# Weight sums of a recursive matrix product: added by accumulating transfers in place of GpSimd, activation differences on VectorE in place of GpSimd

## The chip, the core and the metric

The kernel runs on one core of one Trainium2 chip. The metric is the device time of one execution in microseconds (us); lower is better. Of before there are three timed runs and one profiled execution. Engines are named as in the profile: PE is TensorE (matmuls; PEld its weight loads), DVE is VectorE, ACT is ScalarE, POOL is GpSimd, SP is SyncE, which issues the plain transfers.

## The reference, cut to what matters

One layer of a streaming encoder: attention, a spatial gating branch, a merge, and then a squared-ReLU MLP. All is float32, with 512 tokens and a model width of 2048. The change touches the last product alone:

```
D_MODEL = 2048; SEQ = 512; D_FF = 4 * D_MODEL
h2 = rms_norm(x, g_ff[l])
x = x + jnp.square(jax.nn.relu(h2 @ w_ff1[l])) @ w_ff2[l]
```

`w_ff2` is 8192 x 2048. The kernel computes the product with it by a 2x2 recursive scheme that needs seven block products in place of eight, at the price of sums of weight blocks and differences of activation blocks.

## The kernel before, in words

**Split numbers.** Each float32 operand is split into a high and a low part (`split_to`, L101): ACT casts it to `w_hi` (L103), DVE subtracts that from the operand and gets `w_lo` (L104). A product is then three matmuls (`mm3`, L66 to L70): high by high (L68), low weight by high (L69 for the products named here), high by low (L70). The DVE subtraction needs ACT's cast, and the matmuls need both.

**First product of the MLP.** `hidden` (L597) makes 256 columns of the hidden layer: four loads of `w_ff1` (512 KB each, L87), four splits (L90 on ACT, L92 on DVE), 96 matmuls named `f`, then two evacuations (L603 on DVE, L604 on ACT) into `relu`.

**Second product.** The hidden layer is walked in 16 chunks `f` of 512 rows (L632). For each chunk, `factors` (L610) is called for two pairs of `relu` tiles: four differences of 128x256 each on POOL (L615 to L618, tiles `m`), then seven splits of 128x256 (tiles `ys`, ACT L103 and DVE L104). For each half `g` of the output columns, `strassen` (L140) loads four quarters of a 512x1024 piece of `w_ff2` (512 KB each, L156), and makes seven products of 12 matmuls each (tiles `q`). The names of the products are those of the activation factor: y11, y21, m7, m6, y22, m4, m5. Four of them need a sum of weight quarters, made on POOL (`plus`, L165, 128x1024 each) just ahead of the split: m7 takes w11+w21, m6 that sum and w22 (into a tile of its own, `w_sum`), y22 the latter and w12, m5 w21+w22. Each product is evacuated as soon as its 12 matmuls are done: DVE adds or subtracts the PSUM bank from two or four tiles `x` in SBUF (L643, 128x512). Three of the seven products share one bank, so a bank is read by DVE before the next product that adds to it.

**What sets the order.** Each engine runs its own instructions in order. The program is written in the order just told and then put in order by a scheduler that works from its own estimate of times, so an instruction of a later product can stand ahead of one of an earlier. `ahead` (L638) puts `hidden` of chunk f+1, half g, ahead of `strassen` of chunk f, half g; so PE alternates 96 `f` matmuls and 84 `q` matmuls, and the differences and `ys` splits of chunk f+1 fall into `strassen` of chunk f, g=1. Below, "the g=0 call" and "the g=1 call" are these two. In the last chunk there is no `hidden` left, and the last two calls follow the one before them directly.

**Buffers.** `w_hi` and `w_lo` of both products share six buffers, three pairs (`piece`, and `weight` at L89): the split of a product can begin when the third product before it has left PE. The quarters and `w_sum` share five buffers (`whole`, L590). The raw tiles of `w_ff1` have three of their own.

Of the kernel before, what the change touches and what calls it, by code (L numbers as in the profile page):

```python
# [12 lines left out]
ALU = mybir.AluOpType  # L13
AX = mybir.AxisListType

P = 128
# [11 lines left out]
W = 512  # L28
# [5 lines left out]
def tile_hybrid_layer(ctx: ExitStack, tc: tile.TileContext, x, g_mix, w_in, g_q, g_k, ln_g, ln_b,  # L34
# [4 lines left out]
    nc = tc.nc  # L39
# [10 lines left out]
    def slot(name, dt=F32, pool=slots):  # L50
        return pool.tile([P, 512], dt, name=name, tag="slot")
# [10 lines left out]
    def f32(ap):  # L62
        return ap.bitcast(F32)


    def mm3(o, lh, rh, start, stop, **kw):  # L66

        nc.tensor.matmul(o, lhsT=lh[0], rhs=rh[0], start=start, stop=False, **kw)  # L68
        nc.tensor.matmul(o, lhsT=lh[0], rhs=rh[1], start=False, stop=False, **kw)  # L69
        nc.tensor.matmul(o, lhsT=lh[1], rhs=rh[0], start=False, stop=stop, **kw)  # L70

    state = {"load": None}
# [22 lines left out]
    def split(src, name, scale=None, pool=slots):  # L95

        hi, lo = slot(name + "_hi", F32R, pool), slot(name + "_lo", F32R, pool)
        split_to(hi, lo, src, scale)
        return hi, lo

    def split_to(hi, lo, src, scale=None):  # L101
        if scale is None:
            nc.scalar.copy(out=hi, in_=src)  # L103
            nc.vector.tensor_tensor(out=lo, in0=src, in1=f32(hi), op=ALU.subtract)  # L104
        else:
            nc.scalar.activation(out=hi, in_=src, func=AF.Copy, scale=scale)
            nc.vector.scalar_tensor_tensor(out=lo, in0=src, scalar=scale, in1=f32(hi),
                                           op0=ALU.mult, op1=ALU.subtract)
# [31 lines left out]
    def strassen(wap, r0, c0, lhs, evac):  # L140

        KH = 2

        def piece(name):
            return wpool.tile([P, KH, W], F32R, name=name, tag="w_piece", bufs=6)

        def whole(name):
            return state["whole"].tile([P, KH, W], F32, name=name, tag="whole")

        def quarter(h, c):
            raw = whole("w_raw")
            state["load"] = nc.sync.dma_start(  # L156
                out=raw, in_=wap[r0:r0 + 2 * KH * P, c0 + c * W:c0 + (c + 1) * W]
                .rearrange("(k h p) c -> h p k c", p=P, h=2)[h])
            return raw

        w11, w12, w21, w22 = quarter(0, 0), quarter(1, 0), quarter(0, 1), quarter(1, 1)
        sc = whole("w_sum")

        def plus(o, a, b):
            nc.gpsimd.tensor_tensor(out=o, in0=a, in1=b, op=ALU.add)  # L165


        made = {"m7": lambda: plus(w11, w11, w21), "m6": lambda: plus(sc, w11, w22),
                "y22": lambda: plus(w12, sc, w12), "m5": lambda: plus(w21, w21, w22)}
        take = {"y11": w11, "y21": w12, "m7": w11, "m6": sc, "y22": w12, "m4": w22, "m5": w21}  # L170
        banks = {}
        for name, b, first, last in (("y11", 0, True, False), ("y21", 1, True, True),
                                     ("m7", 2, True, False), ("m6", 0, False, False),
                                     ("y22", 1, True, True), ("m4", 2, False, True),
                                     ("m5", 0, False, True)):
            if name in made:
                made[name]()
            hi, lo = piece("w_hi"), piece("w_lo")
            split_to(hi, lo, take[name])
            if first:  # L180
                banks[b] = [(aux if b == 1 else acc)("q") for _ in range(2)]
            for t in range(2):
                o = banks[b][t]
                for k in range(KH):
                    y = [part[:, t * P:(t + 1) * P] for part in lhs(k, name)]
                    mm3(o, y, (hi[:, k, :], lo[:, k, :]), first and k == 0, k == KH - 1,
                        skip_group_check=True)
                evac(name, t, o)
# [210 lines left out]
    for half in range(2):  # L399
# [4 lines left out]
                 lambda tb, o, v=v: v.append(split(o, "v", rstd[:, tb:tb + 1])), "v")  # L404
# [82 lines left out]
    with tc.issue_after(ref.ins):  # L487
        ws, bs = [], []
        for half in range(2):
            t = slot("ws")  # L490
            nc.sync.dma_start(out=t.rearrange("p (g j) -> p g j", g=4),
                              in_=w_sp[0, half * 4:half * 4 + 4].rearrange("g i j -> i g j"))
# [117 lines left out]
    def factors(act):  # L610

        y11, y12, y21, y22 = act[0][:, :HS], act[0][:, HS:], act[1][:, :HS], act[1][:, HS:]
        ta, tb = slot("m"), slot("m")
        m7, m6, m4, m5 = ta[:, :HS], ta[:, HS:], tb[:, :HS], tb[:, HS:]
        nc.gpsimd.tensor_tensor(out=m7, in0=y12, in1=y22, op=ALU.subtract)  # L615
        nc.gpsimd.tensor_tensor(out=m6, in0=m7, in1=y11, op=ALU.subtract)
        nc.gpsimd.tensor_tensor(out=m4, in0=y21, in1=m6, op=ALU.add)
        nc.gpsimd.tensor_tensor(out=m5, in0=y11, in1=y12, op=ALU.subtract)  # L618
        y = {}
        for name, src in (("y11", y11), ("y21", y21), ("m7", m7), ("m6", m6), ("y22", y22),  # L620
                          ("m4", m4), ("m5", m5)):
            t = slot("ys", F32R)
            y[name] = (t[:, :HS], t[:, HS:])
            split_to(*y[name], src)
        return y
# [6 lines left out]
    for f in range(chunks):  # L632
        ys = [factors(act) for act in ahead]
        ahead = []
        for g in range(2):

            if f < chunks - 1:
                ahead.append(hidden(f + 1, g))  # L638

            def evac_y(name, t, o):  # L640
                for half, c, op in takes[name]:
                    a = x2[2 * half + t, 2 * g + c]
                    nc.vector.tensor_tensor(out=a, in0=a, in1=o, op=op)  # L643
                    if f == chunks - 1 and (name, half, c) in (("m4", 0, 1), ("y21", 0, 0),
                                                              ("m5", 1, 1), ("m5", 1, 0)):
                        tb, j = 2 * half + t, 2 * g + c
                        nc.sync.dma_start(out=out[tb * P:(tb + 1) * P, j * W:(j + 1) * W], in_=a)

            strassen(w_ff2[0], f * PAIRS * 2 * P, g * 2 * W, lambda k, name: ys[k][name], evac_y)
# [25 lines left out]
```

## Time and profile before

| What | Value |
|---|---|
| median of 3 runs | 2575.06 us (2574.0 to 2575.1) |
| the profiled execution's own time | 2574.17 us |
| its span, first to last instruction | 2572.5 us |
| granted PE clock | 1.000 |
| PE busy | 2532.1 us of the span |
| DVE busy | 1438.7 us |
| ACT busy | 852.9 us |
| POOL busy | 589.0 us |
| moved by transfers | 259.83 MB, 101 GB/s on average |

How to read it: a row of a group has the line of the code, the engine, the operation, output and input by name, shape, count, the busy time and the mean duration of one in ns, and behind the bar the idle time just before these instructions with what ended it. In the timeline a row has start, duration, engine and line; a figure in square brackets is the idle time of the engine before it and what ended that. The durations of matmuls overlap, since they are pipelined; their starts follow each other at the true pace. From a transfer's issue to its landing is told by a view of its own.

### The profile page before, as it was taken

Reading aid. Unit: us, or ns where it says so; the run is one execution under the profiler, and the core shown is the slowest. Engines: PE = TensorE matmul, PEld = TensorE weight load, DVE = VectorE, ACT = ScalarE, POOL = GpSimd, SP = SyncE. Lnnn points to the kernel's source line nnn. Section 1 sums busy time; section 2 is a strip of 40 time slices with the busy share of each in tenths; the row PEclk is TensorE's granted clock in tenths of the full one; section 3 lists DMA queues with packets and bytes.
Section 4 is the critical chain, followed back from the end, with each engine's and each line's share of the span. In section 5 each row is a group of like instructions: output and inputs, shape, how many; then the busy total and the mean of one; then the engine's idle time right before and its main releaser. Section 6 shows DMA issues by size and latency. Waiting matters only on the chain.

```text
span 2572.5 us, 28610 instructions
## 1 busy us (share of the span) xinstructions
PE 2532.1 (98%) x11306; PEld 2082.1 (81%) x11306; DVE 1438.7 (56%) x1806; ACT 852.9 (33%) x1172; POOL 589.0 (23%) x379
## 2 busy tenths in 40 slices
PE   8999999999999999999999999999999999999998
PEld 7888888888888888888878777887778777877786
DVE  4555563333335333333475767667666767576759
ACT  5333342222223222223333333333332334233333
POOL 0211110000211000100223242414342333324244
PEclk9999999999999999999999999999999999999999
DMA  5332323333332333434233323233323333332323
GB/s 172 90 91 74 90 64 99 93 97 98 115 115 78 99 101 93 129 107 133 88 110 95 115 87 111 89 115 97 101 90 107 102 95 99 98 115 82 114 68 121
DMA packets 169574, 259.83 MB, mean 101 GB/s; under 512 B 8368, under 2 KB 77024, under 8 KB 169440
## 3 DMA queue, kind: packets, MB, share of 16 engines
q1 hardware_dynamic: 169440, 258.01, 32.7%
q8 instruction: 89, 1.46, 0.2%
q14 instruction: 45, 0.37, 0.0%
HBM read 253.78 MB, written 4.19 MB: 100 GB/s over the span
## 4 chain that ended last, share of the span: by engine, by line
PE 87%; DVE 10%; issue 1%; ACT 1%; DMA 0%; POOL 0%; SPq 0%; DVEq 0%; ACTq 0%; POOLq 0%
PE f L69 9%; PE f L68 9%; PE f L70 9%; PE q L69 6%; PE q L70 6%; PE q L68 6%; DVE w_lo L104 4%; DVE ys L104 3%; DVE x L643 3%; PE xo L70 2%; PE xo L69 2%; PE xo L68 2%; PE gb L68 2%; PE gb L70 2%; PE gb L69 2%; PE ga L68 2%
## 5 line engine op out<-in xcount | busy, mean ns | idle before, releaser
L92 DVE TENSOR_TENSOR w_lo<-w_raw,w_hi 128x1024 fp32r<-128x1024 f32 x336 | 414.2, 1233 | 686.5 <-ACT w_hi L90 677.7
L90 ACT CAST w_hi<-w_raw 128x1024 fp32r<-128x1024 f32 x336 | 353.7, 1053 | 988.8 <-PE q L69 190.0
L104 DVE TENSOR_TENSOR w_lo<-w_raw,w_hi 128x1024 fp32r<-128x1024 f32 x192 | 281.9, 1469 | 255.8 <-ACT w_hi L103 255.8
L68 PE MATMUL f<-h2T_hi,w_hi 128*128 128x512 f32 x1024 | 398.6, 389 | 0.0
L69 PE MATMUL f<-h2T_lo,w_hi 128*128 128x512 f32 x1024 | 398.5, 389 | 0.0
L70 PE MATMUL f<-h2T_hi,w_lo 128*128 128x512 f32 x1024 | 397.9, 391 | 0.0
L69 PE MATMUL q<-w_lo,ys 128*128 128x512 f32 x896 | 352.8, 394 | 26.4 <-DVE w_lo L104 26.3
L165 POOL TENSOR_TENSOR w_raw<-w_raw 128x1024 f32<-128x1024 f32 x64 | 183.1, 2862 | 820.0 <-DVE w_lo L104 820.0
L70 PE MATMUL q<-w_hi,ys 128*128 128x512 f32 x896 | 349.0, 389 | 0.0
L643 DVE TENSOR_TENSOR x<-x,q 128x512 f32<-128x512 f32 x512 | 331.0, 676 | 2.3 <-PE q L70 0.6
L103 ACT CAST w_hi<-w_raw 128x1024 fp32r<-128x1024 f32 x192 | 201.8, 1053 | 391.2 <-PE f L69 290.3
L68 PE MATMUL q<-w_hi,ys 128*128 128x512 f32 x896 | 324.0, 391 | 1.5 <-DVE x L643 1.2
L69 PEld LDWEIGHTS q<-w_lo,ys 128*128 128x128 f32 x896 | 168.1, 188 | 74.1 <-DVE w_lo L104 40.0
L70 PEld LDWEIGHTS f<-h2T_hi,w_lo 128*128 128x128 f32 x1024 | 192.2, 188 | 44.2 <-DVE w_lo L92 4.6
L69 PEld LDWEIGHTS f<-h2T_lo,w_hi 128*128 128x128 f32 x1024 | 192.2, 188 | 40.1
L68 PEld LDWEIGHTS f<-h2T_hi,w_hi 128*128 128x128 f32 x1024 | 192.3, 188 | 39.4
L68 PEld LDWEIGHTS q<-w_hi,ys 128*128 128x128 f32 x896 | 168.1, 188 | 40.3 <-issue 3.5
L70 PEld LDWEIGHTS q<-w_hi,ys 128*128 128x128 f32 x896 | 168.3, 188 | 33.8
L68 PE MATMUL gb<-hT_hi,w_hi 128*128 128x512 f32 x256 | 100.3, 392 | 0.2 <-DVE gb L413 0.2
L68 PE MATMUL xo<-w_hi,mT_hi 128*128 128x512 f32 x256 | 100.5, 393 | 0.0
L68 PE MATMUL ga<-hT_hi,w_hi 128*128 128x512 f32 x256 | 100.4, 392 | 0.0
L69 PE MATMUL ga<-hT_lo,w_hi 128*128 128x512 f32 x256 | 100.0, 391 | 0.0
(199 smaller groups left out, 3919.4 us busy)
## 6 DMA issues: line engine op xcount, KB each, us to landing
w_raw<-in_w_ff_dram SPq DMA_DIRECT2D x256, 512.0 KB, 3.7
w_raw<-in_w_in_dram SPq DMA_DIRECT2D x144, 512.0 KB, 3.7
w_raw<-in_w_out_dram SPq DMA_DIRECT2D x32, 512.0 KB, 3.7
w_raw<-in_w_oa_dram SPq DMA_DIRECT2D x16, 512.0 KB, 3.7
w_raw<-in_w_ob_dram SPq DMA_DIRECT2D x16, 512.0 KB, 3.6
x<-in_x_dram SPq DMA_DIRECT2D x16, 256.0 KB, 5.3
out_dram<-x SPq DMA_DIRECT2D x16, 256.0 KB, 2.2
xq<-in_x_dram SPq DMA_DIRECT2D x12, 256.0 KB, 6.4
```

The lines of the kernel that those rows point to most:

```text
L68: nc.tensor.matmul(o, lhsT=lh[0], rhs=rh[0], start=start, stop=False, **kw)
L69: nc.tensor.matmul(o, lhsT=lh[0], rhs=rh[1], start=False, stop=False, **kw)
L70: nc.tensor.matmul(o, lhsT=lh[1], rhs=rh[0], start=False, stop=stop, **kw)
L90: nc.scalar.copy(out=hi, in_=raw)
L92: nc.vector.tensor_tensor(out=lo, in0=raw, in1=f32(hi), op=ALU.subtract)
L103: nc.scalar.copy(out=hi, in_=src)
L104: nc.vector.tensor_tensor(out=lo, in0=src, in1=f32(hi), op=ALU.subtract)
L165: nc.gpsimd.tensor_tensor(out=o, in0=a, in1=b, op=ALU.add)
L643: nc.vector.tensor_tensor(out=a, in0=a, in1=o, op=op)
```

## The change

`plus` no longer adds two tiles on POOL. It issues a transfer on POOL's queue that reads a quarter of `w_ff2` from memory again and adds it to the destination tile in SBUF (`accum_op=ALU.add`). A tile `sa` is loaded with w11 (a second load of w11, plain, on SP); w21 is added to it (for m7), then, once m7's split has read it, w22 (for m6), then, once m6's split has read it, w12 (for y22). A tile `sb` is loaded with w21, and w22 added to it (for m5). One call thus has five plain loads on SP in place of four, and four accumulating transfers on POOL's queue in place of four POOL additions. The seven products come in another order: m7, y11, y21, m6, m4, y22, m5. The four differences of `factors` move from POOL to DVE.

```diff
+        def rows(h, c):
+            return wap[r0:r0 + 2 * KH * P, c0 + c * W:c0 + (c + 1) * W].rearrange("(k h p) c -> h p k c", p=P, h=2)[h]
...
-        w11, w12, w21, w22 = quarter(0, 0), quarter(1, 0), quarter(0, 1), quarter(1, 1)
-        sc = whole("w_sum")
-
-        def plus(o, a, b):
-            nc.gpsimd.tensor_tensor(out=o, in0=a, in1=b, op=ALU.add)
-
-
-        made = {"m7": lambda: plus(w11, w11, w21), "m6": lambda: plus(sc, w11, w22),
-                "y22": lambda: plus(w12, sc, w12), "m5": lambda: plus(w21, w21, w22)}
-        take = {"y11": w11, "y21": w12, "m7": w11, "m6": sc, "y22": w12, "m4": w22, "m5": w21}
+        def plus(o, h, c):
+
+            nc.gpsimd.dma_start(out=o, in_=rows(h, c), accum_op=ALU.add)
+
+
+        sa, w11, w12 = quarter(0, 0), quarter(0, 0), quarter(1, 0)
+        plus(sa, 0, 1)
+        w22, sb = quarter(1, 1), quarter(0, 1)
+        plus(sb, 1, 1)
+        take = {"y11": w11, "y21": w12, "m7": sa, "m6": sa, "y22": sa, "m4": w22, "m5": sb}
         banks = {}
-        for name, b, first, last in (("y11", 0, True, False), ("y21", 1, True, True),
-                                     ("m7", 2, True, False), ("m6", 0, False, False),
-                                     ("y22", 1, True, True), ("m4", 2, False, True),
+        for name, b, first, last in (("m7", 2, True, False), ("y11", 0, True, False),
+                                     ("y21", 1, True, True), ("m6", 0, False, False),
+                                     ("m4", 2, False, True), ("y22", 1, True, True),
                                      ("m5", 0, False, True)):
-            if name in made:
-                made[name]()
             hi, lo = piece("w_hi"), piece("w_lo")
             split_to(hi, lo, take[name])
+            if name in ("m7", "m6"):
+                plus(sa, 1, 1 if name == "m7" else 0)
...
-        nc.gpsimd.tensor_tensor(out=m7, in0=y12, in1=y22, op=ALU.subtract)
-        nc.gpsimd.tensor_tensor(out=m6, in0=m7, in1=y11, op=ALU.subtract)
-        nc.gpsimd.tensor_tensor(out=m4, in0=y21, in1=m6, op=ALU.add)
-        nc.gpsimd.tensor_tensor(out=m5, in0=y11, in1=y12, op=ALU.subtract)
+        nc.vector.tensor_tensor(out=m7, in0=y12, in1=y22, op=ALU.subtract)
+        nc.vector.tensor_tensor(out=m6, in0=m7, in1=y11, op=ALU.subtract)
+        nc.vector.tensor_tensor(out=m4, in0=y21, in1=m6, op=ALU.add)
+        nc.vector.tensor_tensor(out=m5, in0=y11, in1=y12, op=ALU.subtract)
```

Three places show how the instructions move; all are from the call of chunk f=13, g=1 (the tile numbers differ between the kernels, and the line numbers by one behind L153).

POOL's queue before, in that call: the four sums, then the eight differences of both pairs.

```order
L165 TENSOR_TENSOR w_raw_17260<-w_raw_17260,w_raw_17264 128x1024
L165 TENSOR_TENSOR w_sum_17268<-w_raw_17260,w_raw_17266 128x1024
L165 TENSOR_TENSOR w_raw_17264<-w_raw_17264,w_raw_17266 128x1024
L165 TENSOR_TENSOR w_raw_17262<-w_sum_17268,w_raw_17262 128x1024
L615 TENSOR_TENSOR m_17409<-relu_16977,relu_16980 128x256
L618 TENSOR_TENSOR m_17410<-relu_16977 128x256
```

And now: 17287 is `sa` of this call and 17296 its `sb`; 17619 is `sa` of the next call.

```order
L164 DMA w_raw_17296<-in_w_ff2_dram 128x2x512
L164 DMA w_raw_17287<-in_w_ff2_dram 128x2x512
L164 DMA w_raw_17619<-in_w_ff2_dram 128x2x512
L164 DMA w_raw_17287<-in_w_ff2_dram 128x2x512
L164 DMA w_raw_17628<-in_w_ff2_dram 128x2x512
```

The queue holds transfers alone now, and the third addition to `sa` (the fourth row, for y22) stands behind the first addition to the next call's `sa`.

DVE before, from the two evacuations of `hidden` to the split of m6 (`w_lo` from `w_sum`):

```order
L603 SCALAR_TENSOR_TENSOR relu_17254<-f1_17132,rstd_b_103 128x512
L603 SCALAR_TENSOR_TENSOR relu_17257<-f1_17133,rstd_b_103 128x512
L104 TENSOR_TENSOR w_lo_17311<-w_raw_17260,w_hi_17310 128x1024
L643 TENSOR_TENSOR x2_7982<-x2_7982,q_17273 128x512
L643 TENSOR_TENSOR x2_7984<-x2_7984,q_17274 128x512
L104 TENSOR_TENSOR w_lo_17332<-w_sum_17268,w_hi_17331 128x1024
```

And now, where 17341 is the split of y21 and 17361 that of m6:

```order
L604 SCALAR_TENSOR_TENSOR relu_17281<-f1_17159,rstd_b_103 128x512
L604 SCALAR_TENSOR_TENSOR relu_17284<-f1_17160,rstd_b_103 128x512
L616 TENSOR_TENSOR m_17437<-relu_17003,relu_17006 128x256
L619 TENSOR_TENSOR m_17438<-relu_17003 128x256
L104 TENSOR_TENSOR w_lo_17341<-w_raw_17291,w_hi_17340 128x1024
L617 TENSOR_TENSOR m_17437<-m_17437,relu_17003 128x256
L644 TENSOR_TENSOR x2_8286<-x2_8286,q_17304 128x512
L644 TENSOR_TENSOR x2_8288<-x2_8288,q_17305 128x512
L618 TENSOR_TENSOR m_17438<-relu_17006,m_17437 128x256
L104 TENSOR_TENSOR w_lo_17361<-w_raw_17287,w_hi_17360 128x1024
```

Four differences now stand on DVE ahead of m6's split; the evacuations in between are m7's where they were y11's.

PE before, where y22 begins (17350 is its `w_hi`, 17331 that of m6): it follows on the whole of m6.

```order
L69 MATMUL q_17274<-w_lo_17332,ys_16843 128x512
L70 MATMUL q_17274<-w_hi_17331,ys_16843 128x512
L68 MATMUL q_17354<-w_hi_17350,ys_16819 128x512
L68 MATMUL q_17355<-w_hi_17350,ys_16819 128x512
L69 MATMUL q_17354<-w_lo_17351,ys_16819 128x512
```

And now (17397 is y22's `w_hi`, 17360 m6's, 17379 m4's):

```order
L68 MATMUL q_17304<-w_hi_17379,ys_16848 128x512
L68 MATMUL q_17305<-w_hi_17379,ys_16848 128x512
L68 MATMUL q_17325<-w_hi_17360,ys_16842 128x512
L69 MATMUL q_17325<-w_lo_17361,ys_16842 128x512
L70 MATMUL q_17325<-w_hi_17360,ys_16842 128x512
L68 MATMUL q_17325<-w_hi_17360,ys_16869 128x512
L69 MATMUL q_17325<-w_lo_17361,ys_16869 128x512
L70 MATMUL q_17325<-w_hi_17360,ys_16869 128x512
L68 MATMUL q_17401<-w_hi_17397,ys_16845 128x512
L69 MATMUL q_17304<-w_lo_17380,ys_16848 128x512
```

y22's first matmul is now the 51st of the call: 48 of m7, y11, y21 and m6 and two of m4 stand ahead of it, and m4's other ten behind it. In the g=0 call it is the 61st, behind the whole of m4.

More of the change, by code (lines that the diff above doesn't have):

```diff
@@ L152, in whole @@
             return state["whole"].tile([P, KH, W], F32, name=name, tag="whole")
+        def rows(h, c):
+            return wap[r0:r0 + 2 * KH * P, c0 + c * W:c0 + (c + 1) * W].rearrange("(k h p) c -> h p k c", p=P, h=2)[h]
         def quarter(h, c):
             raw = whole("w_raw")
-            state["load"] = nc.sync.dma_start(
-                out=raw, in_=wap[r0:r0 + 2 * KH * P, c0 + c * W:c0 + (c + 1) * W]
-                .rearrange("(k h p) c -> h p k c", p=P, h=2)[h])
-            return raw
-        w11, w12, w21, w22 = quarter(0, 0), quarter(1, 0), quarter(0, 1), quarter(1, 1)
-        sc = whole("w_sum")
-        def plus(o, a, b):
-            nc.gpsimd.tensor_tensor(out=o, in0=a, in1=b, op=ALU.add)
-        made = {"m7": lambda: plus(w11, w11, w21), "m6": lambda: plus(sc, w11, w22),
-                "y22": lambda: plus(w12, sc, w12), "m5": lambda: plus(w21, w21, w22)}
-        take = {"y11": w11, "y21": w12, "m7": w11, "m6": sc, "y22": w12, "m4": w22, "m5": w21}
+            state["load"] = nc.sync.dma_start(out=raw, in_=rows(h, c))
+            return raw
+        def plus(o, h, c):
[5 more added lines that the diff above has]
+        take = {"y11": w11, "y21": w12, "m7": sa, "m6": sa, "y22": sa, "m4": w22, "m5": sb}
         banks = {}
-        for name, b, first, last in (("y11", 0, True, False), ("y21", 1, True, True),
-                                     ("m7", 2, True, False), ("m6", 0, False, False),
-                                     ("y22", 1, True, True), ("m4", 2, False, True),
+        for name, b, first, last in (("m7", 2, True, False), ("y11", 0, True, False),
+                                     ("y21", 1, True, True), ("m6", 0, False, False),
+                                     ("m4", 2, False, True), ("y22", 1, True, True),
                                      ("m5", 0, False, True)):
-            if name in made:
-                made[name]()
             hi, lo = piece("w_hi"), piece("w_lo")
             split_to(hi, lo, take[name])
+            if name in ("m7", "m6"):
+                plus(sa, 1, 1 if name == "m7" else 0)
             if first:
```

## The prediction

> **What bounds the kernel now.** I read the page first, then the waits of PE, then single stretches. All below is one profiled execution of 2574.17 us, 1.67 us more than its span; the median of the runs is 0.9 us above it.
>
> ```profile
> span 2572.5 us, 28610 instructions
> PE 2532.1 (98%) x11306; PEld 2082.1 (81%) x11306; DVE 1438.7 (56%) x1806; ACT 852.9 (33%) x1172; POOL 589.0 (23%) x379
> ```
>
> PE is the bound; the change leaves its matmuls as they are, so it can only give back PE's idle 40 us or add to them. The waits of PE from 1300 us to the end, which is the MLP:
>
> ```profile
> PE q L69 <- DVE w_lo L104: 26.3, 34, 1.8
> PE q L68 <- DVE x L643: 1.2, 1, 1.2
> PE q L68 <- ACT w_hi L103: 0.2, 1, 0.2
> ```
>
> So 27.7 us of waits (26.3 + 1.2 + 0.2) stand in `strassen`. Where they are: stages of the MLP (length, PE, PEld, DVE, ACT and POOL busy, then clock and DMA), and PE's two waits in one g=1 call.
>
> ```profile
> 1400.00:1500.00 100.00, 98.48 (x432) 80.58 (x431) 67.69 (x83) 36.46 (x52) 45.17 (x25) 1.00 0.30 92
> 1500.00:1600.00 100.00, 96.96 (x422) 78.33 (x421) 73.95 (x98) 38.40 (x54) 32.24 (x20) 1.00 0.33 100
> ```
>
> ```profile
> 2009.02 0.50 PE L69 MATMUL q<-w_lo,ys 128*128 128x512 f32 x1 [0.94 <-DVE w_lo L104]
> 2012.96 0.50 PE L69 MATMUL q<-w_lo,ys 128*128 128x512 f32 x1 [0.57 <-DVE w_lo L104]
> ```
>
> Each g=1 call loses 1.51 us, the g=0 call nothing (the stretch with one g=1 call lacks 1.52 us, the one with two 3.04). Chunks 0 to 14 lose 15 x 1.51 = 22.7 us, and the last two calls, with no `hidden` ahead, the other 5.0.
>
> Why DVE is late: these are DVE and POOL in that call.
>
> ```profile
> 1997.70 2.03 DVE L104 TENSOR_TENSOR w_lo<-w_raw,w_hi 128x1024 fp32r<-128x1024 f32 x1 [0.22 <-ACT w_hi L103]
> 1998.61 1.73 POOL L615 TENSOR_TENSOR m<-relu 128x256 f32<-128x256 f32 x1
> 2002.03 0.95 DVE L104 TENSOR_TENSOR ys<-relu,ys 128x256 fp32r<-128x256 f32 x1
> 2003.51 0.41 DVE L104 TENSOR_TENSOR ys<-relu,ys 128x256 fp32r<-128x256 f32 x1
> ```
>
> Beside a POOL instruction a DVE subtraction takes up to 0.95 us instead of 0.41. The groups of 1400 to 2540 us say the same of all of them:
>
> ```profile
> L104 DVE TENSOR_TENSOR w_lo<-w_raw,w_hi 128x1024 fp32r<-128x1024 f32 x166 | 243.3, 1465 | 228.0 <-ACT w_hi L103 228.0
> L92 DVE TENSOR_TENSOR w_lo<-w_raw,w_hi 128x1024 fp32r<-128x1024 f32 x104 | 126.7, 1218 | 59.8 <-ACT w_hi L90 59.8
> L615 POOL TENSOR_TENSOR m<-relu 128x256 f32<-128x256 f32 x28 | 37.8, 1350 | 0.0
> L617 POOL TENSOR_TENSOR m<-relu,m 128x256 f32<-128x256 f32 x28 | 22.5, 805 | 2.2
> L165 POOL TENSOR_TENSOR w_sum<-w_raw 128x1024 f32<-128x1024 f32 x28 | 68.1, 2432 | 2.2
> ```
>
> L104 and L92 are the same subtraction, 1465 ns beside POOL's sums and 1218 ns mostly without them.
>
> **Part by part.** *POOL's arithmetic goes.* 128 sums and 128 differences leave POOL. DVE gains about 0.25 us on each of some 190 subtractions (1465 - 1218 ns), 47 us. It gets 128 differences of 0.41 us (a 128x256 subtraction without POOL, above), 52 us. With both, DVE stays at about 70% of the MLP, so only the place of the differences counts, below. The 27.7 us of waits can go. What is late next is the weight sum.
>
> *The chain of sums.* Four accumulates per call are new; three of them hang on each other through `sa`. (All steps here are worked out from the rows below: 0.228 us per matmul, 2.4 us per split.) The second starts after m7's split, whose buffers come free two products of 24 `f` matmuls ahead of m7 (48 x 0.228 = 10.9 us), so about 8.5 us ahead of m7's matmuls; m6 is needed 36 x 0.228 = 8.2 us behind their start. `sb` is used last. The first has half a period: its buffer is the first to come free, with y11's split of the call before. That split ends 24 x 0.228 - 2.4 = 3 us ahead of m7's matmuls, and the load for it lands 3.7 us later. The third is tight: it can't be issued before m6's split has read `sa`, and y22 needs it. In POOL's queue it stands behind the first accumulate of the next call, issued, by the above, 5 us earlier; I cost that at nothing, and if the load came later than that, its delay would be passed on whole.
>
> The time that it has, with PE's first m7 matmul at zero. DVE's steps, from the starts of instructions that follow each other:
>
> ```profile
> 2006.49 0.67 DVE L643 TENSOR_TENSOR x<-x,q 128x512 f32<-128x512 f32 x1
> 2007.09 0.74 DVE L104 TENSOR_TENSOR ys<-m,ys 128x256 fp32r<-128x256 f32 x2
> 2007.76 1.21 DVE L104 TENSOR_TENSOR w_lo<-w_raw,w_hi 128x1024 fp32r<-128x1024 f32 x1
> 2008.89 0.67 DVE L643 TENSOR_TENSOR x<-x,q 128x512 f32<-128x512 f32 x1
> ```
>
> ```profile
> L103 ACT CAST w_hi<-w_raw 128x1024 fp32r<-128x1024 f32 x167 | 175.6, 1053 | 337.9 <-PE f L69 258.7 <-PE q L69 58.0 <-PE q L70 13.6
> ```
>
> A 512-wide step is 0.60, a 256-wide 0.34 (0.67 for two), a 1024-wide 1.13 and done after 1.21. In the g=1 call DVE has, from about 0.2 on: the second relu 0.60, two differences 0.67, y21's split 1.13, a difference 0.34, two evacuations 1.20, a difference 0.34, m6's split 1.21. That is 5.7 us. PE's step is 0.228 (98.48 us for 432), so y22's first matmul, the 51st, is due at 50 x 0.228 = 11.4. ACT's cast of 1.05 and about 0.2 for hand-overs come before. The accumulate has 11.4 - 1.25 - 5.7 = 4.4 us from issue to landing. In the g=0 call no differences stand there: m6's cast waits for m7's twelve matmuls (2.7, and 0.2 until they are done), so its split ends at about 2.9 + 1.05 + 1.2 = 5.2; y22's `w_lo` is due at the 63rd matmul, 62 x 0.228 = 14.1, less the cast, the subtraction and hand-overs 2.5. That leaves 6.4; since PE has a little more to do first I take 6.5.
>
> So with T the time of an accumulate, PE loses per chunk (T - 4.4) in the g=1 call and (T - 6.5) in the g=0 call, where positive.
>
> *How long is T?* No such transfer is in the trace. Nearest rows: the DMA totals, the plain load of the same 512 KB (us from issue to landing), and its issue on SP (min, median, max in ns).
>
> ```profile
> q1 hardware_dynamic: 169440, 258.01, 32.7%
> w_raw<-in_w_ff_dram SPq DMA_DIRECT2D x256, 512.0 KB, 3.7
> L156 SPq DMA_DIRECT2D w_raw<-in_w_ff_dram x128: 367/368/469, 1215.6 to 2540.4; - x128
> ```
>
> The transfer engines move 258.01 MB in 32.7% of 2572.5 us, 307 GB/s, so 0.524 MB take 1.7 of the 3.7 us. An accumulate must read the old tile as well. Bound below: that read hides behind the one from memory, T = 3.7, and POOL issues as fast as SP. Bound above: two whole transfers, 7.4, and an issue as long as POOL's longest row, 2.4 for 0.37: T = 9.4. In between: the second read takes engine time again, 3.7 + 1.7 = 5.4; POOL's issue costs 1.35 (its L615, the middle of its three rows) instead of 0.37: **T = 6.4**. I take that, nearest to the plain load with each new piece once.
>
> By the Trainium skill, Collectives: The Full Stack, the section on the bandwidth ceiling, an add in a transfer is slow for its two source reads on one ring and not for the arithmetic; no row here shows it, and the sum by it would be the one I take. By the Trainium skill, DMA: Bandwidth & Descriptors, the section on the anatomy of one DMA, a transfer issued by GpSimd takes about 2.0 us and its bytes at 436 GB/s, which gives an estimate of 4.4 us for 512 KB read twice, and with it the first rival's time; the plain load's 3.7 us here is already above that formula's 3.2 for it.
>
> *The sum.* At T = 6.4 the g=1 calls of 15 chunks lose 15 x 2.0 = 30 us, the g=0 calls nothing, the last two calls 5 as before (between 2 and 8: two places like the above and no `hidden`). 35 - 27.7 = +7.3 us on 2574.17, which is 2581.5; on the median 2575.06 about 2582.4. Traffic: one load and four accumulates replace nothing, so 9 transfers in place of 4 per call, with the accumulates counted twice (5 + 8 + 4 of `w_ff1` = 17 for 8) the transfer engines go from 33% to about 70% busy in the MLP. A collision can add up to 1.7 us to an accumulate; that is in the upper end.
>
> **The rivals.** *A, the sums land in time.* The old tile is read while memory's data come; POOL's issue is short. T is at most 4.9. For it: 2.0 of the load's 3.7 us are not engine time and needn't be paid twice. Against it: the issue by software. All waits of before go; by my estimate some 0.7 us per chunk stay, since DVE's queue in the g=1 call is longer by 8 x 0.34 us, and 3 at the end: 15 x 0.7 + 3 - 27.7 = -14, 2561. It decides from T = 5.9 downward, where 15 x 1.5 + 5 = 27.5 equals the waits of before.
>
> *B, the one pays for the other.* T between 5.6 and 6.25 gives -5 to +5 us, 2575.
>
> *C, the additions go one after the other.* The engines read, add and write each 2 KB row without overlap, or the 70% of traffic is in the way: T = 9.4. 15 x (5.0 + 2.9) + 10 - 27.7 = +101, 2676. At T = 8.0 it is 15 x (3.6 + 1.5) + 8 - 27.7 = +57, 2632.
>
> *D, the differences on DVE do the harm.* They are 1.35 us of the 5.7 above. Without them the g=1 call would have 5.75 us for T, so at T = 6.4 they are 20 of the 30 us; with T small they cost nothing, as then only PE's order counts. This is within the forecast and A, and no case of its own.
>
> **How the numbers follow.** A difference under 0.2%, 5 us, can't be told from none. The forecast has T from 6.25 to 8, slower: 0.38. C has T above 8: 0.12. B: 0.18. A and what lies between it and B: 0.32. Rows that leave T between 3.7 and 9.4 allow no more. The range begins at 2558, a little under A, where no gain is left, and ends at 2635, T = 8.1; beyond lies the 0.12 of C and little else.
>
> **What would show it.** Right: POOL's arithmetic gone from the MLP; L104 on `w_lo` at 1.22 us instead of 1.47; PE's waits at y22's first matmul (L68, for `w_hi` on ACT, and ACT's for the transfer), about 2 us, once per chunk in the g=1 call; the time from m6's split to the landing about 6.4 us. Wrong: waits at y22 in both calls (C), or none of over 0.7 us (A); PE waiting at m7 or m6 would mean that the first or second accumulate or the queue's order counts, which I cost at nothing; PE waiting for `x` (L644) or `ys` would mean that DVE, not the transfer, is the bound.

## The result, and the profile after

The changed kernel takes **2608.76 us** (median of 4 runs, 2599.66 to 2614.15); the kernel before took 2574.53 us beside it (2573.51 to 2575.1). The ratio is 1.013 with a 95% interval of 1.0101 to 1.0159: slower by 34 us. The forecast was 2582 in a range of 2558 to 2635, with "slower" as the likeliest sign. The sign and the place of the loss were right, the size was about a fifth of the measured one (7 us for 34).

The profiled execution took 2609.81 us. Its page, span, engines and the two transfer queues (packets, MB, share of 16 engines):

```profile
span 2608.1 us, 28749 instructions
PE 2541.8 (97%) x11306; PEld 2089.9 (80%) x11306; DVE 1395.9 (54%) x1934; ACT 844.8 (32%) x1172; POOL 272.9 (10%) x251
...
q1 hardware_dynamic: 178144, 274.79, 33.4%
q0 software_dynamic: 34816, 67.12, 16.6%
...
w_raw<-in_w_ff_dram SPq DMA_DIRECT2D x288, 512.0 KB, 4.6
...
w_raw<-in_w_ff_dram POOLq DMA_DIRECT2D x128, 512.0 KB, 6.2
```

The work that was to leave POOL has left it, 589.0 us down to 272.9, and VectorE has become a little less busy (1438.7 to 1395.9). Neither shortens the execution by itself, since PE is the bound. What is new stands in the last row: an accumulate takes 6.2 us from issue to landing, the plain load beside it 4.6 where it was 3.7.

The waits of PE from 1300 us to the end:

```profile
PE q L68 <- ACT w_hi L103: 46.0, 30, 3.9
PE q L69 <- DVE w_lo L104: 6.8, 14, 0.5
```

52.8 us where 27.7 stood. Before, the waits were for VectorE (`w_lo`); now they are for ACT's `w_hi`, and ACT is not the cause: it is waiting itself. One wait in a g=1 call, followed back from PE (third row) to ACT (second) and to the issue on POOL (first):

```profile
2018.70 1.20 POOL L164 DMA_DIRECT2D w_raw<-in_w_ff_dram  x1 [3.75 <-DVE w_lo L104]
...
2024.80 2.00 ACT L103 CAST w_hi<-w_raw 128x1024 fp32r<-128x1024 f32 x2 [5.25 <-DMA w_raw<-in_w_ff_dram]
2025.89 0.50 PE L68 MATMUL q<-w_hi,ys 128*128 128x512 f32 x1 [1.70 <-ACT w_hi L103]
```

POOL issues the third accumulate as soon as m6's split has read `sa`; 6.1 us later (2024.80 - 2018.70) ACT can cast; PE has stood for 1.70 us at y22's first matmul. So y22's cast was due 4.4 us after the issue (6.1 - 1.70), which is the budget that the prediction gave.

The PE time itself went up as well, 2532.1 to 2541.8, for the same matmuls. In stretches of 5 us (length, PE, PEld, DVE, ACT, POOL, then the granted clock):

```profile
2110.00:2115.00 5.00, 4.33 (x12) 3.42 (x13) 4.36 (x8) 3.25 (x8) 0.00 (x0) 0.66 0.48 163
2115.00:2120.00 5.00, 5.00 (x24) 4.11 (x23) 5.00 (x11) 2.57 (x4) 1.20 (x1) 1.00 0.49 133
```

```profile
2200.00:2205.00 5.00, 5.00 (x17) 3.96 (x16) 5.00 (x11) 3.24 (x9) 0.00 (x0) 0.68 0.54 148
2205.00:2210.00 5.00, 5.00 (x24) 4.13 (x23) 5.00 (x8) 2.00 (x3) 1.20 (x1) 1.00 0.58 170
...
2290.00:2295.00 5.00, 5.00 (x24) 4.14 (x23) 5.00 (x11) 2.05 (x5) 0.46 (x1) 1.00 0.50 163
```

The first rows of both fences lie right behind a wait, of 2.34 us at 2110.67 and of 3.34 us at 2199.33. The clock granted there is 0.66 and 0.68; PE is busy all the time in 2200 to 2205 but does 17 matmuls where 24 go into 5 us, which is 7 x 0.228 = 1.6 us lost a second time. Behind the wait of 1.70 us at 2025.89 and one of 2.78 us at 2286.53 (last row) the clock stays at 1.00. The trace's record of the clock has six such drops in the MLP before PE's last matmul, to 0.50, five of 3.41 us and one of 6.83; that is 11.9 us of work at most, less what of it lies inside a wait. So the span's 35.6 us (2608.1 - 2572.5) are 25.1 of waits, 9.7 of PE's own time and 0.8 of the rest.

### The profile page after: what moved, and what is told of

It reads as the page before. It is cut to its first block, busy times and chain, and to the rows that moved or that the text cites. A ratio compares the mean times of both kernels' runs of the same rounds, so it can differ in the third digit from the quotient of the medians.

```text
span 2608.1 us, 28749 instructions
## 1 busy us (share of the span) xinstructions
PE 2541.8 (97%) x11306; PEld 2089.9 (80%) x11306; DVE 1395.9 (54%) x1934; ACT 844.8 (32%) x1172; POOL 272.9 (10%) x251
## 3 DMA queue, kind: packets, MB, share of 16 engines
q0 software_dynamic: 34816, 67.12, 16.6%
## 4 chain that ended last, share of the span: by engine, by line
PE 80%; DMA 10%; DVE 5%; issue 2%; ACT 2%; POOL 0%; ACTq 0%; SPq 0%; DVEq 0%; POOLq 0%
DMA w_raw<-in_w_ff_dram 9%; PE f L70 9%; PE f L68 9%; PE f L69 9%; PE q L69 4%; PE q L70 4%; PE q L68 4%; DVE w_lo L104 3%; PE xo L70 2%; PE xo L68 2%; PE xo L69 2%; PE gb L68 2%; PE gb L69 2%; PE gb L70 2%; PE ga L68 2%
## 5 line engine op out<-in xcount | busy, mean ns | idle before, releaser
L92 DVE TENSOR_TENSOR w_lo<-w_raw,w_hi 128x1024 fp32r<-128x1024 f32 x336 | 414.6, 1234 | 658.6 <-ACT w_hi L90 649.7
L90 ACT CAST w_hi<-w_raw 128x1024 fp32r<-128x1024 f32 x336 | 353.7, 1053 | 926.0 <-PE q L69 138.5
L104 DVE TENSOR_TENSOR w_lo<-w_raw,w_hi 128x1024 fp32r<-128x1024 f32 x224 | 273.9, 1223 | 331.5 <-ACT w_hi L103 331.1
L103 ACT CAST w_hi<-w_raw 128x1024 fp32r<-128x1024 f32 x224 | 232.3, 1052 | 573.2 <-PE f L69 296.3
L70 PE MATMUL f<-h2T_hi,w_lo 128*128 128x512 f32 x1024 | 391.5, 389 | 0.0
L68 PE MATMUL q<-w_hi,ys 128*128 128x512 f32 x896 | 334.5, 398 | 46.3 <-ACT w_hi L103 46.3
L70 PE MATMUL q<-w_hi,ys 128*128 128x512 f32 x896 | 353.2, 394 | 0.0
L164 POOL DMA_DIRECT2D w_raw<-in_w_ff_dram x128 | 154.8, 1213 | 1395.3 <-DVE w_lo L104 487.8
```

The lines of the kernel that those rows point to most:

```text
L90: nc.scalar.copy(out=hi, in_=raw)
L92: nc.vector.tensor_tensor(out=lo, in0=raw, in1=f32(hi), op=ALU.subtract)
L164: nc.gpsimd.dma_start(out=o, in_=rows(h, c), accum_op=ALU.add)
```

## The experiments

The theory to be tested: the third accumulate is waited for, because it can only start behind m6's split and y22 comes soon after; its time is set by reading the old tile. Rivals: the differences on VectorE delay m6's split; the traffic of the transfers is in the way; the accumulates as such are dear. The first four kernels ran beside each other on one chip (before there: 2573.94 us, 2573.47 to 2574.54), the last three beside each other (before there: 2574.26, 2573.12 to 2574.73).

**Sums only: the four differences back on GpSimd.** The edit, on the changed kernel:

```diff
-        nc.vector.tensor_tensor(out=m7, in0=y12, in1=y22, op=ALU.subtract)
+        nc.gpsimd.tensor_tensor(out=m7, in0=y12, in1=y22, op=ALU.subtract)
...
```

> The changed kernel with the four differences back on GpSimd (line numbers as after). My theory: PE waits for y22's weight sum, the third accumulate, which takes 6.1 to 6.8 us from issue to landing where 4.4 us are there in the g=1 call. Without the differences on DVE, m6's split ends up to 1.35 us earlier there, so the 15 long waits (34 us in all) shrink by 0.7 to 1.35 us each, less what GpSimd's differences slow DVE's subtractions (0.95 for 0.41 us), and the waits over 2.3 us behind which the clock falls become few: 2580 to 2600. Rival, traffic: the 70% busy transfer engines are the harm as such, and nothing moves: 2609. Rival, the differences on DVE are the harm: all of it goes, 2560 to 2575.

Measured: 2614.15 us, ratio 1.0154 (1.0139 to 1.0169). That is above the 2580 to 2600 of the theory, and no gain from a shorter queue on VectorE: the interval of this ratio overlaps that of the changed kernel (1.0101 to 1.0159), so the two can't be told apart. The waits of PE from 1300 us on:

```profile
PE q L68 <- DVE x L644: 29.3, 15, 2.2
PE q L68 <- ACT w_hi L103: 12.6, 10, 7.6
PE q L69 <- DVE w_lo L104: 9.1, 23, 0.5
```

The wait for the accumulate is mostly gone, 46.0 to 12.6, but a wait for the evacuation of a product (`x`) has come in its place, 15 times, once per chunk. What makes the evacuation late, in one g=1 call:

```profile
2020.97 1.20 POOL L164 DMA_DIRECT2D w_raw<-in_w_ff_dram  x1
...
2021.75 1.20 POOL L616 TENSOR_TENSOR m<-relu 128x256 f32<-128x256 f32 x1
2021.83 2.78 DVE L104 TENSOR_TENSOR ys<-relu,ys 128x256 fp32r<-128x256 f32 x1
...
2022.45 1.18 POOL L619 TENSOR_TENSOR m<-relu 128x256 f32<-128x256 f32 x1
...
2023.14 1.18 POOL L617 TENSOR_TENSOR m<-m,relu 128x256 f32<-128x256 f32 x1
...
2026.07 0.67 DVE L644 TENSOR_TENSOR x<-x,q 128x512 f32<-128x512 f32 x1
...
2026.80 0.79 PE L68 MATMUL q<-w_hi,ys 128*128 128x512 f32 x1 [2.13 <-DVE x L644]
```

A 128x256 subtraction on VectorE that takes 0.41 us alone took 2.78 us beside POOL's differences and the issue of an accumulate. So the differences on VectorE are not what harms the changed kernel; taken off it they only exchange one wait for another of about the same size. (Two kernels below keep them on VectorE and run at 2550 us.)

**Differences only: the kernel before, with the four differences on VectorE.** The edit, on the kernel before:

```diff
-        nc.gpsimd.tensor_tensor(out=m7, in0=y12, in1=y22, op=ALU.subtract)
+        nc.vector.tensor_tensor(out=m7, in0=y12, in1=y22, op=ALU.subtract)
...
```

> The kernel before with only the differences moved to DVE; the weight sums stay on GpSimd. My theory: the differences cost DVE 2.7 us per chunk which nothing waits for, and DVE is no longer slowed by GpSimd's differences while it does the ys subtractions, which is what made the two waits of 1.51 us in each g=1 call: 2550 to 2570. Rival, the differences on DVE are the harm of the change: slower than before, 2580 to 2600.

Measured: 2557.18 us, ratio 0.9935 (0.992 to 0.995). This half of the change alone is a gain of 17 us. Its waits of PE from 1300 us on:

```profile
PE q L69 <- DVE w_lo L104: 13.0, 19, 0.8
PE q L68 <- DVE x L643: 4.8, 2, 3.4
```

17.8 us for 27.7: half of the waits for VectorE's `w_lo` came from POOL's differences (26.3 to 13.0). The other half is left while the sums are on POOL; that the sums cause it was not tried by itself. The two halves of the change do not add up: +40 us for the sums alone and -17 for the differences alone make +23, and together they are +34.

**y22 last: the changed kernel with y22 behind m5.** The product that needs the third accumulate comes at the end of its call; the last store of block (1, 0) moves with it.

```diff
-                                     ("m4", 2, False, True), ("y22", 1, True, True),
-                                     ("m5", 0, False, True)):
+                                     ("m4", 2, False, True), ("m5", 0, False, True),
+                                     ("y22", 1, True, True)):
```

> The changed kernel with one thing else: y22 is made last, after m5 (the block that it completes is stored after it). T and the traffic stay. My theory: 12 more matmuls stand ahead of y22, so the third accumulate has 2.7 us more, about 7.1 us in the g=1 call and over 9 in the g=0 call; the waits for it fall from 34 to under 8 us in the g=1 calls and to none in the g=0 calls, the clock stays at 1.00, some 10 us of short waits for DVE remain: 2560 to 2575. Rival, traffic or the differences on DVE: nothing moves, 2600 to 2615. Rival, the next sum in the chain becomes late in its place (m6 or the first one of the next call): 2590 or more, with waits at another product.

Measured: 2550.72 us, ratio 0.991 (0.9895 to 0.9925): 58 us faster than the changed kernel, 23 us faster than the kernel before, and some 9 us under the range of the theory. The waits of PE from 1300 us on, and the accumulates on the page (count, KB each, median us to landing):

```profile
PE q L68 <- ACT w_hi L103: 9.8, 7, 4.6
PE q L69 <- DVE w_lo L104: 1.4, 1, 1.4
PE q L68 <- DVE x L644: 0.2, 1, 0.2
```

```profile
PE 2524.2 (99%) x11306; PEld 2085.4 (82%) x11306; DVE 1394.5 (55%) x1934; ACT 849.6 (33%) x1172; POOL 272.8 (11%) x251
...
w_raw<-in_w_ff_dram POOLq DMA_DIRECT2D x128, 512.0 KB, 6.0
```

The accumulates are as many and take about as long, 6.0 us for 6.2, and 41.4 of the 52.8 us of waits are gone, since twelve more matmuls lie between m6's split and y22. PE's own time fell with the waits, 2541.8 to 2524.2. So it is neither the accumulates as such nor their traffic, but this one accumulate's place ahead of y22.

**Plain transfers: the changed kernel with the additions left out.** The same transfers by the same queue, without the sum; what comes out of the second product is another result.

```diff
-            nc.gpsimd.dma_start(out=o, in_=rows(h, c), accum_op=ALU.add)
+            nc.gpsimd.dma_start(out=o, in_=rows(h, c))
```

> The changed kernel with all four accumulates replaced by plain transfers of the same bytes on the same queue, with the same waits; it leaves out the additions of weights. My theory: without the read of the old tile T falls by about 1.7 us to 4.5 us, which is about what the g=1 call has; the waits for y22 fall to under 10 us in all, the transfer engines to some 52% busy: 2560 to 2570. Rival, the issue by software is the cost and the addition is free: T stays at 6.2 and the time at 2609. Rival, DVE: waits for DVE stay and the time is over 2590.

Measured: 2545.48 us, ratio 0.9891 (0.9874 to 0.9907), some 15 us under the range of the theory. Of the waits of PE from 1300 us on 5.0 us are left. The queue and the issue of this run, the page first, then the groups of 1400 to 2500 us:

```profile
q0 software_dynamic: 18432, 67.12, 8.0%
...
w_raw<-in_w_ff_dram POOLq DMA_DIRECT2D x128, 512.0 KB, 4.0
```

```profile
L164 POOL DMA_DIRECT2D w_raw<-in_w_ff_dram x108 | 78.2, 724 | 1021.5 <-DVE w_lo L104 411.6 <-DVE relu L604 213.7 <-DVE x L644 161.1
```

The group after, over 1400 to 2540 us:

```profile
L164 POOL DMA_DIRECT2D w_raw<-in_w_ff_dram x107 | 128.8, 1204 | 1018.2 <-DVE w_lo L104 395.8 <-DVE x L644 294.0 <-DVE relu L604 171.0
```

With the addition the same 67.12 MB take nearly twice the packets (34816 for 18432) and twice the engines' time (16.6% for 8.0%), the issue 1.20 us for 0.72, and the landing 6.2 us for 4.0. The addition is thus 2.2 us of the 6.2; issue by software instead of on SP is nearly nothing (4.0 for the 3.7 of the load before). At 4.0 us the third transfer is inside its budget of 4.4, and the waits go. (This run halves the traffic of the accumulates too, so it can't part the transfer's time from the traffic; the run with y22 last, at full traffic, does.)

**Third sum on POOL: the changed kernel with y22's weights added up by GpSimd.** `sa`, finished for m6, is added to y21's tile; two accumulates on `sa` are left.

```diff
-        take = {"y11": w11, "y21": w12, "m7": sa, "m6": sa, "y22": sa, "m4": w22, "m5": sb}
+        take = {"y11": w11, "y21": w12, "m7": sa, "m6": sa, "y22": w12, "m4": w22, "m5": sb}
...
-                plus(sa, 1, 1 if name == "m7" else 0)
+                if name == "m7":
+                    plus(sa, 1, 1)
+                else:
+                    nc.gpsimd.tensor_tensor(out=w12, in0=sa, in1=w12, op=ALU.add)
```

> The changed kernel with one accumulate of three turned back: GpSimd adds the finished sum in `sa` to the tile of y21's weights, and y22 is split from that; m7's and m5's accumulates stay. Theory (it is the third accumulate that is waited for, 6.1 to 7.7 us where 4.4 to 6.5 us are there): the waits of TensorE for ACT's `w_hi` of y22, some 46 us in the profile after, go nearly to nothing, and the 9.7 us by which TensorE's own time had grown go with them; the addition on GpSimd takes some 2.4 us and slows VectorE a little. That gives 2548 to 2562. Rival 1 (accumulates as such are dear, whichever is waited for): two of three are left, so about two thirds of the loss stay, some 2590 to 2600. Rival 2 (the wait goes over to the evacuation of y11, as when the differences were on GpSimd, because GpSimd's additions slow VectorE): 2580 to 2600 with waits for VectorE's `x` in place of those for `w_hi`.

Measured: 2550.09 us, ratio 0.9908 (0.9891 to 0.9924), as the theory had it. The waits of PE from 1290 us on, and the addition in one call, 2.40 us where the accumulate takes 6 to 8:

```profile
PE q L69 <- DVE w_lo L104: 7.3, 16, 0.9
PE q L68 <- ACT w_hi L103: 3.1, 3, 2.0
```

```profile
2025.29 2.40 POOL L183 TENSOR_TENSOR w_raw<-w_raw 128x1024 f32<-128x1024 f32 x1 [0.17 <-DVE w_lo L104]
```

Three of the four accumulates per call are still there and cost nothing to be seen. No wait for `x` came up in place of the old one, and PE's own time is 2523.3 us.

**The third accumulate twice.** A second addition of the same rows to `sa`, behind the first.

```diff
                 plus(sa, 1, 1 if name == "m7" else 0)
+            if name == "m6":
+                plus(sa, 1, 0)
```

> The changed kernel with the third accumulate issued twice in a row, so that y22's weights get one term twice: the kernel computes something else there. Theory: from issue to cast it takes about 12.4 us instead of 6.2 to 7.7; each of the some 33 waits grows by about 6 us, so by 190 to 210 us in sum. If a wait of over 2.3 us lowers the granted clock behind it, as the windows of the profile after suggest, nearly every one of these waits now does so, at 1 to 2 us each: TensorE's busy time, 2541.8 us after, rises by a further 25 to 50 us, and the time is 2830 to 2870. Rival (the clock has nothing to do with the waits): TensorE's busy time stays within 5 us of 2541.8 or falls, and the time is 2795 to 2820. Rival (GpSimd's issue time is what costs, not the transfer): 34 more issues of 1.2 us, some 2650.

Measured: 2820.58 us, ratio 1.0962 (1.0945 to 1.0978). The page, and the waits from 1290 us on:

```profile
PE 2600.8 (92%) x11306; PEld 2128.4 (76%) x11306; DVE 1404.6 (50%) x1934; ACT 842.4 (30%) x1172; POOL 311.4 (11%) x283
```

```profile
PE q L68 <- ACT w_hi L103: 205.1, 33, 13.8
```

33 waits of 6.2 us in the mean; they grew by 152 us in all (205.1 for the 52.8 after), less than the 190 to 210 expected. PE's own time grew by 59 us, a little more than the 25 to 50 expected and clearly not by the rival's 5 at most. The time stands 10 us under the theory's range and just above the rival's 2820, so by the total alone the two would hardly be told apart; PE's busy time does. Over the 2532.1 of the kernel before it is 68.7 us, or 2.1 us for each of the 33 waits. One place, behind a wait of 6.42 us that ended at 2049.33:

```profile
2050.00:2055.00 5.00, 4.96 (x17) 3.62 (x16) 5.00 (x11) 4.38 (x8) 0.00 (x0) 0.73 0.35 107
2055.00:2060.00 5.00, 5.00 (x24) 4.14 (x23) 5.00 (x8) 1.06 (x1) 1.20 (x1) 1.00 0.75 221
```

The same picture as behind the waits of the changed kernel: 17 matmuls for 24, at a granted clock of 0.73. The issue on POOL as the cause (2650) is refuted.

**Both: y22 last and its sum on POOL.** The two edits above together. Three accumulates per call stay, two of them on `sa`.

> y22 as the last product of its call, and its sum made by GpSimd from the finished `sa`: two accumulates per call are left. By the theory y22 as last product leaves only waits at the program's end (8.4 us of the 11.4 in the run with y22 last alone), and a GpSimd addition of 2.4 us in place of a transfer of 6 us takes some of these away: 2543 to 2552, against 2550.72 with y22 last alone. Rival: GpSimd's addition slows VectorE's subtractions and evacuations as its differences did, which would show as waits for VectorE, and the time is 2555 to 2570.

Measured: 2561.19 us, ratio 0.9951 (0.9936 to 0.9966): some 10 us slower than either edit alone, outside the theory's range and inside the rival's. The waits of PE from 1290 us on, and VectorE's subtraction in the groups of 1400 to 2500 us:

```profile
PE q L69 <- DVE w_lo L104: 10.6, 16, 1.6
PE q L68 <- DVE x L647: 6.1, 17, 1.4
PE q L68 <- ACT w_hi L103: 1.1, 1, 1.1
```

```profile
L104 DVE TENSOR_TENSOR w_lo<-w_raw,w_hi 128x1024 fp32r<-128x1024 f32 x187 | 239.7, 1282 | 220.2 <-ACT w_hi L103 220.2
```

The waits for the third sum fell to 1.1 us, as they should, but small waits for VectorE came instead, 16.7 us in all. The subtraction takes 1.28 us beside POOL's addition where it took 1.22 after. With y22 last there was nothing left for POOL to win in the chunks, only its price to pay. That GpSimd's slowing of VectorE is the whole of that price was not tried; the run only shows whom PE waits for.

## Why the prediction was right, and where its size was off

*The mechanism held.* The third accumulate was named as the tight one, y22's first matmul as the place, ACT's `w_hi` as what is waited for, and once per chunk in the g=1 call as the count. The waits are there, 15 of them, of 1.70 to 3.34 us and 34.0 us in all, and moving y22 or taking that one accumulate away removes them.

That the time lies inside the range is in part luck: the range's upper end was held for slower accumulates, and 9.7 us of what fills it are the clock, which no term had.

*What was costed at nothing was nothing.* The first two accumulates of `sa` and that of `sb` cost no wait that shows: with the third one replaced, three per call stay and the kernel runs at 2550.09 us. POOL's queue in front of the third one cost nothing either (POOL stood idle for 3.75 us before it, in the row above).

*VectorE's terms held.* The prediction had 1.22 us for the subtraction without POOL beside it, and about 70% of the MLP for VectorE. In the changed kernel's groups and in one window:

```profile
L104 DVE TENSOR_TENSOR w_lo<-w_raw,w_hi 128x1024 fp32r<-128x1024 f32 x186 | 227.5, 1223 | 289.5 <-ACT w_hi L103 289.3
...
L619 DVE TENSOR_TENSOR m<-relu 128x256 f32<-128x256 f32 x28 | 11.8, 420 | 0.0
```

```profile
1400.00:2500.00 1100.00, 1059.67 (x4597) 865.68 (x4597) 710.42 (x1025) 375.94 (x514) 123.99 (x103) 0.99 0.65 158
```

1223 ns, a difference of 0.42 us for the 0.41 taken, 65% of the stretch, and transfer engines at 0.65 for the 70% worked out. Two readings were a little off, and nothing hangs on them: 28 of the some 190 subtractions (those of m6's sum) took 1274 ns before, so the gain is nearer 42 us than 47; and POOL's longest row before was not 2432 ns but 2875 (the sums into `w_raw`).

*The first term that was mis-sized: T as one number.* T = 6.4 is near the page's median of 6.2, and its parts were about right: 0.83 us for the longer issue (1.20 - 0.37) where 0.98 was taken, and with it 2.5 us in all above the plain load of 3.7, where 2.7 was taken. But T is not the same everywhere. From the start of POOL's issue to ACT's cast it is 6.1 to 7.7 us in the fifteen g=1 calls, 6.66 in the mean, and 6.1 to 8.2 in the g=0 calls, 7.54 in the mean of fourteen (each from a pair of rows like POOL's and ACT's above). The prediction named a collision of up to 1.7 us and left it to the upper end of the range; in the g=0 calls it was the rule. In the g=0 call a plain load is issued into the accumulate's time, 2.4 us behind it (2063.24):

```profile
2060.80 1.20 POOL L164 DMA_DIRECT2D w_raw<-in_w_ff_dram  x1 [3.23 <-DVE w_lo L104]
...
2063.24 7.05 SPq L159 DMA_DIRECT2D w_raw<-in_w_ff_dram  x2
2067.60 2.00 ACT L103 CAST w_hi<-w_raw 128x1024 fp32r<-128x1024 f32 x2 [5.64 <-DMA w_raw<-in_w_ff_dram]
```

In the g=1 call the next plain load comes 5.1 us behind the issue. The run with the accumulate twice bears this out by a difference that it had not been made for: its second accumulates take 5.8 to 6.2 us from issue to cast where no plain load was issued within 2 us of them, and 6.0 to 8.2 where one was, 0.9 to 1.8 us ahead. The neighbouring load is not all of it: in the g=1 calls the plain loads are issued at the same distances each time (3.3 us ahead, 5.1 behind) and the time still goes from 6.1 to 7.7 us, and one g=0 call with a load 1.8 us behind the issue takes 6.1 us. A kernel that keeps the loads away from the accumulates was not tried.

With these T the prediction's own formula gives what was measured. The g=1 calls: 15 x (6.66 - 4.4) = 33.9 us, measured 34.0, predicted 30. The g=0 calls: 14 x (7.54 - 6.5) = 14.6, measured 11.7, predicted nothing. The last two calls: measured 7.1, predicted 5. Together 52.8 for the predicted 35: this is 18 of the missing 28 us. Waits at y22 in both calls were the prediction's own sign for rival C; they came, but at accumulates of 6.1 to 8.2 us and not at C's 8 and more throughout, and the time is far from C's 2632 to 2676.

*The second term was not there at all: the clock.* Of the rest 9.7 us are PE's own time. The sum took 0.228 us per matmul whatever happens ahead of it. A long wait costs a second time, at a lower granted clock behind it; the doubled accumulate, at 33 waits of 6.2 us, raised PE's time by a further 59 us.

*When the clock drops.* The six drops begin at times that lie whole multiples of 3.41 us apart (2111.04 and 2199.79 for instance, 26 x 3.413). With the execution cut into such periods, each drop begins at the end of a period in which PE was idle for 2.3 us or more, and no drop follows a period with 1.8 or less. The wait of 2.34 us lies inside one period (2107.63 to 2111.04); the one of 2.78 us lies across two, with 1.37 us in the first and 1.41 in the second. In the sums-only kernel a wait of 1.82 us (ended at 1767.05), all inside one period, was followed by a drop, and one period with 1.91 us of idle time was not. So in these traces it is the idle time within a period that counts, and about 1.8 to 2.0 us of it are enough. By the Trainium skill, TensorE: Matmul & The Clock Gate, the section on HAM oscillation, gaps of PE above some 3.4 us are to be avoided, as the clock falls back to half behind them. The half agrees with the rows here (17 of 24 matmuls, as from about 3 us at half the clock); the threshold doesn't: drops stood behind waits of 2.34 and 1.82 us.

*A remark that was wrong: rival D.* It said that without the differences on VectorE 20 of the g=1 calls' 30 us would go. With the differences on GpSimd the waits for the accumulate did fall, but the product two places ahead was evacuated late instead, and the kernel was no faster (2614.15 for 2608.76 us). The step that failed is the one that priced VectorE's queue as if its instructions kept their time when GpSimd works beside them. The rival of traffic (C) has its part in the g=0 calls.

*A wait costs more than it is listed with.* PE's busy time is 2524.2 us with y22 last and 2532.1 before, at a full granted clock in the chunks of both. The edges of the waits are about as much. A wait is counted from the end of the matmul ahead of it, 0.39 us behind its start, where the next one would otherwise start after 0.23; and the first matmul behind the wait holds PE for 0.34 us. The wait of 1.70 us at 2025.89 is an example: 2.08 us from start to start (2023.81 to 2025.89), and the next start is 0.34 us later. Over the waits of the MLP this sums to 13.2 us before (37 waits) and to 4.4 us with y22 last (16 waits); the difference of 8.8 us is a little over the 8, and y22 last has one drop of the clock near its end (6.8 us from 2515.32).

*What stays open.* Why an accumulate takes 6.1 us in one g=1 call and 7.7 in another is not known. Nor is it shown why PE is kept waiting for `w_lo` in the kernel before once POOL's differences are gone (13.0 us).

## What to carry to other kernels

A sum by accumulating transfers is cheap as long as nobody waits for it: here it freed GpSimd and VectorE, and what it cost was one link of a chain that could start only when a buffer had been read and was needed 4.4 us later. Before such a change, work out for the last link when it can be issued and when its product is due, at the transfer's time under load and not at its median; then put the product that needs it last, or make that one sum elsewhere (2550.72 and 2550.09 us here, for 2574 before and 2608.76 as the change stood). One of the two is enough, and a wait of PE is to be counted at more than its listed length: some 0.3 us at its edges, and from about 2 us on the clock as well.

## What the runs showed of the hardware

- An accumulate of 512 KB from memory lands in 5.9 to 6.2 us (medians of the runs), a plain transfer by the same queue in 4.0, one by SP's queue in 3.7 in the kernel before and 3.9 to 4.6 beside accumulates. It takes 1.9 times the packets, 2.1 times the transfer engines' time, and 1.20 us of POOL for its issue instead of 0.72.
- The granted clock drops to 0.50 for 3.41 us or a multiple of it. In these traces a drop began at the end of a period of 3.41 us in which PE was idle for 1.8 us at the least; 1.95 us of idle time was the most that stayed without one. A drop of 3.41 us costs up to 1.7 us, and 33 waits of 6.2 us raised PE's busy time by 2.1 us each.
- A wait of PE costs some 0.3 us more than its listed length (13.2 us at 37 waits before, 4.4 us at 16 with y22 last).
- Beside three differences on GpSimd of some 1.2 us each and the issue of an accumulate, a VectorE subtraction of 0.41 us took 2.78 us.
